# Where the split weights and the activations begin within a line of 256 bytes of SBUF

## The chip, the cores and the metric

The kernel runs on one core of a Trainium2 chip. The time is device microseconds of one execution of the whole program. Before the change three runs took 1443.82, 1444.29 and 1444.64 us, so the median is 1444.29 us.

## The reference, cut to what matters

A decoder layer of 256 tokens and 2048 channels, all in float32: one input projection that feeds sliding-window attention and a state-space mixer side by side, an output projection, and a convolved, gated feed-forward layer.

```python
def reference(x, ...):
    h = x
    h = h + _hybrid_mixer(_rmsnorm(h, norm_mix), w_in, ..., w_out)
    h = h + _conv_ffn(_rmsnorm(h, norm_ffn), w_up, ffn_conv_w, ffn_conv_b, w_down)
    return _rmsnorm(h, norm_final)

def _hybrid_mixer(xn, w_in, ..., w_out):
    proj = xn @ w_in                      # [256, 2048] @ [2048, 9248]
    ...
    return jnp.concatenate([attn, y], axis=-1) @ w_out      # [256, 4096] @ [4096, 2048]

def _conv_ffn(hn, w_up, ffn_conv_w, ffn_conv_b, w_down):
    u = _causal_dwconv(hn @ w_up, ffn_conv_w, ffn_conv_b)   # [256, 2048] @ [2048, 11264]
    gate, val = u[..., :D_FF], u[..., D_FF:]
    return (jax.nn.silu(gate) * val) @ w_down               # [256, 5632] @ [5632, 2048]
```

## The kernel before, in words

Nearly all of the work is four large products of activations with weights, and each is made of three: an operand is split into a rounded part `hi` and the rest `lo` (type float32r), and hi x hi, hi x lo and lo x hi are summed in PSUM (`mm3`, lines 155 to 158). The weights come from HBM by SP's queue in blocks of 128 x 2048 floats into one of three buffers `raw` (`pieces`, line 77). Each half of a block is then split (`split`, line 67): ScalarE (ACT) casts it to `hi` (line 70), VectorE (DVE), or for one half in four GpSimd (POOL), subtracts `hi` from `raw` into `lo` (line 72). `hi` and `lo` have four buffers each, taken in turn, 4352 bytes a partition, of which a half of 1024 floats uses 4096.

A matmul has a stationary operand of 128 columns, loaded by a weight load ahead of it, and a moving operand of up to 512 columns. There are two forms:

- `gemm_tok` (line 174) has the activations stationary and the weights moving, 512 columns at a time. It serves the keys and the time steps (`w_kd`, in two cuts of 256 and 288 columns), the values, the queries and z (activations in `xT`), the output projection (`attT`, then `yT`) and, written out separately (`down`, line 835), the down projection (`gs`). Leaving `w_kd` aside these are 864 matmuls on `xT` (9 products of 16 row tiles x 2 token tiles x 3), 768 on `attT` and `yT` and 1056 on `gs`.
- `gemm_chan` (line 200) has the weights stationary and the activations moving. In the state space (lines 217 to 219) it makes 1536 matmuls of 256 columns of `xT`. In the up projection (lines 223 and 225) a 512-column matmul on `hi` (the activation's `hi` and `lo` beside each other) and a 256-column one on `lo` make a pair; there are 1408 pairs on `h2T`, which has the buffer of `xT`.

An activation's tile holds for each of 16 row tiles a `hi` of 256 floats and a `lo` of 256 floats. Every slice that a matmul of a large product reads begins a multiple of 256 bytes after the start of its tile, except the second row tile of a part of `w_kd`, which begins 2176 bytes after the first. So an operand's place within a line of 256 bytes is that of its tile.

The tiles' starts are set by the pools, which allot a partition's bytes in the order of the calls. In the built program, in bytes past a multiple of 256: `xT` and `h2T` 128; all buffers of `hi` and `lo` 96 (their spacing, 4352, is 17 x 256); `attT`, `yT` and `gs` 96; in attention `vs` 160 and `pt` and `po` 96.

The mixers' smaller steps (attention, the state space's chunks) are called in between the large products' turns (`later`, `step`), and a scheduler of the tile framework sets the order on each engine from its own estimate of time.

Of the kernel before, what the change touches and what calls it, by code (L numbers as in the profile page):

```python
# [36 lines left out]
RAWW = 4 * KDT  # L37
# [10 lines left out]
def hymba(ctx, tc, x, xt, w_kd, w_in, w_out, w_up, w_down, par, vecs, gfin, con, out):  # L48
# [16 lines left out]
    share = [0, 0]  # L65

    def split(raw, o, n):
        hi = wp.tile([P, RAWW // 2], F32R, tag="hi", name="hi", bufs=4)
        lo = wp.tile([P, RAWW // 2], F32R, tag="lo", name="lo", bufs=4)
# [7 lines left out]
    def pieces(src, width, parts, load=None, work=None):  # L77
        """the parts of a block's splits; load, work: what goes before a part's load and split."""
        raw = wp.tile([P, RAWW], F32, tag="raw", name="raw", bufs=3)
        n = width // parts  # L80
        if load:
            for h in range(parts):
                load(h)
                SY.dma_start(out=raw[:, h * n : (h + 1) * n], in_=src[:, h * n : (h + 1) * n])
        else:
            SY.dma_start(out=raw[:, :width], in_=src)
        out = []
        for h in range(parts):
            if work:
                work(h)  # L90
            out.append(split(raw, h * n, n))
        return out

    xT = cp.tile([P, NKT, 2, S], F32R, tag="xT", name="xT")
# [22 lines left out]
    def rstd(dst, ss, n):  # L117
        """dst = (ss / n + EPS) ** -0.5, a column for each of the token tiles."""
# [4 lines left out]
    def rows_of(dst, r):  # L123
        """dst[p, t] = r of token t, on every partition."""
# [7 lines left out]
    def split_T(dst, kt, src, g, view=lambda a: a):  # L132
        """dst[:, kt] = the two parts of src * g."""
# [6 lines left out]
    def transpose_split(src, ct0, dst, kt0, n, gbase):  # L140
        """src [tokens, t, channels] to the parts of its transpose, n channel tiles times their weights."""
# [18 lines left out]
    # work beside the large products: steps that come up so many turns after they are called for  # L160
# [13 lines left out]
    def gemm_tok(blocks, actT, evac, width=2048, cuts=((0, 512),), tag="acc", parts_of=None):  # L174
        """out[token, column]: activations stationary, weights moving."""
# [24 lines left out]
    def gemm_chan(blocks, actT, evac, tag="acc", wide=True):  # L200
        """out[channel, token]: weights stationary, activations moving; wide: in two sums for evac to add."""
# [29 lines left out]
    def conv(dst, b, rB, wcol, bias, taps, wide):  # L231
        """dst = causal convolution over tokens of b * rB, channels on partitions."""
# [15 lines left out]
    attT = mixctx.enter_context(tc.tile_pool(name="mp0", bufs=1)).tile([P, NKT, 2, S], F32R, name="attT")  # L248

    # =========== attention ===========  # L250
# [675 lines left out]
def _cols(v):  # L926
    """[..., n * P] to [P, ... * n]."""
    return v.reshape(-1, P).T
# [61 lines left out]
```

## Time and profile before

| | |
|---|---|
| median of three runs | 1444.29 us (1443.82 to 1444.64) |
| span of the profiled execution, first to last instruction | 1442.0 us |
| TensorE busy (matmuls) | 1406.4 us of the span |
| weight loads / VectorE / ScalarE / GpSimd busy | 1231.3 / 989.6 / 772.0 / 269.4 us |
| HBM read | 259.92 MB, 182 GB/s over the span |

The profile gives no time of the profiled execution but its span, so the time that lies around the span is taken as 1444.29 - 1442.0 = 2.3 us. Stages by TensorE's lines: keys, values and queries from 6 us, attention's and the state space's products to 525 us, output projection to 703 us, up projection to 1193 us, down projection to 1432 us. In a row of the profile a matmul's duration is longer than the time until the next one starts, because matmuls overlap; the difference of two starts is called its spacing here.

### The profile page before, as it was taken

To read this page: it belongs to the slowest core of one execution; us is meant where nothing else is said; L and a number is where in the kernel's file an instruction comes from. 1 tells how busy PE (TensorE), PEld (TensorE's weight loads), DVE (VectorE), ACT (ScalarE), POOL (GpSimd) and SP (SyncE) were. 2 spreads that over 40 slices of the span, in tenths; PEclk is the share of its full clock that TensorE was granted. 3 is DMA by queue.
4 is the path that set the end of the run, shared out by engine and by line. 5 is a ranking of instruction groups with operands and counts; after the bars stand their busy time and mean duration, and the time that the engine had idled before them with its cause. 6 is when DMAs were issued, how large, how long until landed. Compare 5 with 4: busy or idle time off the path is not lost.

```text
span 1442.0 us, 20476 instructions
## 1 busy us (share of the span) xinstructions
PE 1406.4 (98%) x7925; PEld 1231.3 (85%) x7925; DVE 989.6 (69%) x1454; ACT 772.0 (54%) x1209; POOL 269.4 (19%) x187
## 2 busy tenths in 40 slices
PE   8999999899999999999999999999999999999997
PEld 8888888789999988888888888888888888888886
DVE  6579999788685755555577776867767767545555
ACT  6565677456555554344465554555555554444444
POOL 0124544443434330000000111101111001000001
PEclk9999999999999999999999999999999999999999
DMA  8643333445545456554655555555555455555552
GB/s 317 237 166 125 117 118 117 140 153 190 182 172 186 155 175 257 179 201 175 226 180 195 187 181 200 187 193 190 190 187 192 176 204 190 190 204 182 197 199 94
DMA packets 40561, 263.37 MB, mean 183 GB/s; under 512 B 4608, under 2 KB 5248, under 8 KB 10640
## 3 DMA queue, kind: packets, MB, share of 16 engines
q1 hardware_dynamic: 38560, 254.69, 49.4%
q0 software_dynamic: 1904, 7.37, 1.8%
q8 instruction: 62, 1.02, 0.3%
q14 instruction: 35, 0.29, 0.1%
HBM read 259.92 MB, written 2.13 MB: 182 GB/s over the span
## 4 chain that ended last, share of the span: by engine, by line
PE 81%; DVE 10%; ACT 3%; issue 3%; POOL 1%; DMA 1%; SPq 0%; DVEq 0%; POOLq 0%; ACTq 0%
PE acc L225 11%; PE aux L225 11%; PE acc L158 10%; PE acc L157 10%; PE acc L156 10%; PE aux L223 6%; PE acc L223 6%; PE aux L156 3%; PE aux L157 3%; PE aux L158 3%; DVE lo L72 3%; DVE u L242 2%; PE acc L219 1%; PE acc L218 1%; PE acc L217 1%
## 5 line engine op out<-in xcount | busy, mean ns | idle before, releaser
L72 DVE TENSOR_TENSOR lo<-raw,hi 128x1024 fp32r<-128x1024 f32 (+2 forms) x442 | 550.0, 1250 | 348.9 <-ACT hi L70 348.3
L70 ACT CAST hi<-raw 128x1024 fp32r<-128x1024 f32 (+2 forms) x474 | 492.2, 1047 | 451.7 <-PE acc L158 135.3
L225 PE MATMUL acc<-h2T,hi 128*128 128x512 f32 x704 | 243.4, 391 | 0.0
L225 PE MATMUL aux<-h2T,hi 128*128 128x512 f32 x704 | 243.0, 391 | 0.0
L223 PE MATMUL aux<-h2T,lo 128*128 128x256 f32 x704 | 191.1, 282 | 0.0
L223 PE MATMUL acc<-h2T,lo 128*128 128x256 f32 x704 | 191.0, 282 | 0.0
L225 PEld LDWEIGHTS aux<-h2T,hi 128*128 128x128 f32 x704 | 129.8, 188 | 24.6
L225 PEld LDWEIGHTS acc<-h2T,hi 128*128 128x128 f32 x704 | 129.8, 188 | 24.5
L217 PE MATMUL acc<-xT,hi 128*128 128x256 f32 x512 | 145.4, 285 | 0.0
L218 PE MATMUL acc<-xT,hi 128*128 128x256 f32 x512 | 144.7, 283 | 0.0
L219 PE MATMUL acc<-xT,lo 128*128 128x256 f32 x512 | 143.9, 282 | 0.0
L817 POOL TENSOR_TENSOR gT<-gate,cv 128x256 f32<-128x256 f32 x44 | 61.2, 1392 | 434.5 <-DVE cv L242 424.0
L223 PEld LDWEIGHTS acc<-h2T,lo 128*128 128x128 f32 x704 | 132.9, 189 | 3.9
L223 PEld LDWEIGHTS aux<-h2T,lo 128*128 128x128 f32 x704 | 132.9, 189 | 3.8
L156 PE MATMUL acc<-hi,xT 128*128 128x512 f32 (+1 forms) x320 | 117.6, 387 | 6.4 <-ACT hi L70 5.7
L157 PE MATMUL acc<-lo,xT 128*128 128x512 f32 (+1 forms) x320 | 122.5, 386 | 0.6 <-DVE lo L72 0.6
L158 PE MATMUL acc<-hi,xT 128*128 128x512 f32 (+1 forms) x320 | 122.1, 384 | 0.0
L72 POOL TENSOR_TENSOR lo<-raw,hi 128x1024 fp32r<-128x1024 f32 x32 | 82.7, 2584 | 146.3 <-ACT hi L70 146.2
L218 PEld LDWEIGHTS acc<-xT,hi 128*128 128x128 f32 x512 | 97.1, 190 | 0.4
L217 PEld LDWEIGHTS acc<-xT,hi 128*128 128x128 f32 x512 | 97.0, 190 | 0.4
L219 PEld LDWEIGHTS acc<-xT,lo 128*128 128x128 f32 x512 | 96.9, 190 | 0.2
L156 PEld LDWEIGHTS acc<-hi,xT 128*128 128x128 f32 x320 | 60.4, 195 | 17.1 <-ACT hi L70 5.7
(224 smaller groups left out, 2421.9 us busy)
## 6 DMA issues: line engine op xcount, KB each, us to landing
raw<-in_w_up SPq DMA_DIRECT2D x88, 1024.0 KB, 4.8
raw<-in_w_in SPq DMA_DIRECT2D x68, 1024.0 KB, 4.8
raw<-in_w_down SPq DMA_DIRECT2D x44, 1024.0 KB, 4.8
raw<-in_w_out SPq DMA_DIRECT2D x32, 1024.0 KB, 4.8
e<-acs_d POOLq DMA_DIRECT2D x8, 512.0 KB, 6.2
raw<-in_w_kd SPq DMA_DIRECT2D x6, 544.0 KB, 7.8
x_r<-in_x SPq DMA_DIRECT2D x2, 1024.0 KB, 5.3
h<-in_x POOLq DMA_DIRECT2D x4, 512.0 KB, 7.5
```

The costliest lines, as they stand in the source:

```text
L70: A.copy(out=hi[:, :n], in_=raw[:, o : o + n])
L72: (G if share[0] and share[1] % share[0] == 0 else V).tensor_tensor(out=lo[:, :n], in0=raw[:, o : o + n], in1=hi[:, :n].bitcast(F32), op=A ...
L156: PE.matmul(out=o, lhsT=lh, rhs=rh, start=first, stop=False)
L157: PE.matmul(out=o, lhsT=lh, rhs=rl, start=False, stop=False)
L158: PE.matmul(out=o, lhsT=ll, rhs=rh, start=False, stop=last)
L217: PE.matmul(out=b[ct][:, :S], lhsT=wh, rhs=rh, start=kt == 0, stop=False)
L218: PE.matmul(out=b[ct][:, :S], lhsT=wh, rhs=actT[:, kt, 1, :], start=False, stop=False)
L219: PE.matmul(out=b[ct][:, :S], lhsT=wl, rhs=rh, start=False, stop=end)
L223: PE.matmul(out=b[ct][:, :S], lhsT=wl, rhs=rh, start=False, stop=False)
L225: PE.matmul(out=b[ct], lhsT=wh, rhs=actT[:, kt, :, :], start=kt == 0, stop=end)
L242: V.scalar_tensor_tensor(out=dst[:, j:], in0=u[:, : S - j], scalar=wcol(taps - 1 - j), in1=dst[:, j:], op0=ALU.mult, op1=ALU.add,)
L817: G.tensor_tensor(out=gT[:, i, :], in0=gate[:, ct, :], in1=dst, op=ALU.mult)
```

## The change

The tiles of the large products get places of their own. A new helper `placed` allots a tile on a line of 256 bytes with some bytes to spare and returns the part that begins `at` bytes in. The four buffers of `hi` (and of `lo`) become four tiles of one buffer each, at 0, 64, 128 and 192; `hi` and `lo` of the same half have the same place. `xT` begins at 0, and `h2T`, `attT`, `yT` and `gs` at 32.

```diff
-RAWW = 4 * KDT
+RAWW = 2048
+HALF = 1024
+LINE = 256
+
+W_AT, X_AT, H_AT, M_AT = (0, 64, 128, 192), 0, 32, 32
...
+    def placed(pool, n, at, tag, **kw):
+        tl = pool.tile([P, n + at // 4], F32R, tag=tag, align_bytes=LINE, **kw)
+        return tl[:, at // 4 : at // 4 + n]
+
     def split(raw, o, n):
-        hi = wp.tile([P, RAWW // 2], F32R, tag="hi", name="hi", bufs=4)
-        lo = wp.tile([P, RAWW // 2], F32R, tag="lo", name="lo", bufs=4)
+        j = share[1] % len(W_AT)
+        hi = placed(wp, HALF, W_AT[j], f"hi{j}", name="hi", bufs=1)
+        lo = placed(wp, HALF, W_AT[j], f"lo{j}", name="lo", bufs=1)
...
     def pieces(src, width, parts, load=None, work=None):
-        raw = wp.tile([P, RAWW], F32, tag="raw", name="raw", bufs=3)
         n = width // parts
+        per = RAWW // n
+        raws = [wp.tile([P, RAWW], F32, tag="raw", name="raw", bufs=3) for _ in range(-(-parts // per))]
+        at = lambda h: raws[h // per][:, h % per * n : (h % per + 1) * n]
...
-    xT = cp.tile([P, NKT, 2, S], F32R, tag="xT", name="xT")
+    def acts(pool, at, **kw):
+        return placed(pool, NKT * 2 * S, at, **kw).rearrange("p (k i s) -> p k i s", i=2, s=S)
+
+    xT = acts(cp, X_AT, tag="xT", name="xT")
...
     def parts_kd(i, src):
-        n = 1 if i == 0 else 2
+        n = 1
...
-        return pieces(src, 4 * KDT, 4 if i == 0 else 2, load, work)
+        return pieces(src, 4 * KDT, 4, load, work)
...
-        ta, tb, tcc, td = (ap.tile([P, nd], F32, tag=f"sp{i}", name=f"sp{i}") for i in range(4))
+        ta, tb, tcc, td = (ap.tile([P, nd], F32, tag=t, name=t, bufs=1) for t in ("sp0", "sp1", "rpa", "rpb"))
...
-        gs = fp.tile([P, 2, S], F32R, tag="gs", name="gs", bufs=4)
+        gs = placed(fp, 2 * S, M_AT, "gs", name="gs", bufs=4).rearrange("p (i s) -> p i s", i=2)
```

`attT` and `yT` change like `gs` (`M_AT`), `h2T` like `xT` (`H_AT`). A buffer of `raw` shrinks from 2176 to 2048 floats and one of `hi` or `lo` from 1088 to 1024, which makes room. For this the blocks of `w_kd`, of 2176 floats, are now all loaded and split in quarters of 544, three in one `raw` buffer and the fourth in another; before, the first block came in quarters and the other three in halves. Two small tiles of `steps_dt` share buffers with those of `rope`.

In the built program the tiles stand where the change says: the buffers of `hi` and `lo` at 0, 64, 128 and 192, `xT` at 0, `h2T`, `attT`, `yT` and `gs` at 32; `vs` is now at 96, and `pt` and `po` at 32.

The places that matter for a matmul are those of its moving operand and of the next stationary operand, whose load runs beside it. Below, the **distance** is the first minus the second, in bytes, taken around the line of 256:

| form | distance before | distances after, by buffer of the weights |
|---|---|---|
| `gemm_tok` on `xT`, 512 columns | 224 | 0, 64, 128, 192 |
| `gemm_tok` on `attT`, `yT`; `down` on `gs`, 512 columns | 0 | 224, 32, 96, 160 |
| `gemm_chan` on `xT`, 256 columns | 32 | 0, 192, 128, 64 |
| `gemm_chan` on `h2T`, 512 and 256 columns | 32 | 32, 224, 160, 96 |
| attention's values: `pt` or `po` moving, `vs` stationary, 256 columns | 192 | 192 |

The order of the instructions changes in the first third of the program. On SP's queue, at the second block of `w_kd` (`xraw` takes four row tiles of the input, `raw` the weights; a number tells the buffer's use), before:

```order
L84 DMA raw_105<-in_w_kd 128x544
L312 DMA xraw_92<-in_xt 128x512
L84 DMA raw_186<-in_w_kd 128x1088
L312 DMA xraw_92<-in_xt 128x512
L84 DMA raw_186<-in_w_kd 128x1088
L319 DMA con_t_70<-in_con 128x576
```

and now, at its last two quarters:

```order
L327 DMA xraw_92<-in_xt 128x256
L96 DMA raw_187<-in_w_kd 128x544
L327 DMA xraw_92<-in_xt 128x256
L96 DMA raw_188<-in_w_kd 128x544
L334 DMA con_t_70<-in_con 128x576
```

Each half became two quarters, and the fourth quarter goes to a `raw` buffer of its own. On TensorE, at the first queries (`aux <- con_t, q_t` are their transposes, put in between the matmuls of the next product), before:

```order
L156 MATMUL acc_784<-hi_791,xT_69 128x512
L442 MATMUL aux_833<-con_t_70,q_t_615 128x128 x4
L157 MATMUL acc_784<-lo_792,xT_69 128x512
L158 MATMUL acc_784<-hi_791,xT_69 128x512
L156 MATMUL acc_783<-hi_850,xT_69 128x512
```

and now:

```order
L171 MATMUL acc_824<-hi_831,xT_69 128x512
L172 MATMUL acc_824<-lo_832,xT_69 128x512
L457 MATMUL aux_873<-con_t_70,q_t_655 128x128 x4
L173 MATMUL acc_824<-hi_831,xT_69 128x512
L171 MATMUL acc_823<-hi_890,xT_69 128x512
```

The transposes moved back by one matmul. There are more such moves, by one to a few matmuls, up to the last products of the state space; from the output projection on, TensorE's order is the same.

## Rows read from the trace of the kernel before

**Rows 1.** The page: span, engines' busy time, shares of the chain that ended last.

```profile
span 1442.0 us, 20476 instructions
...
PE 1406.4 (98%) x7925; PEld 1231.3 (85%) x7925; DVE 989.6 (69%) x1454; ACT 772.0 (54%) x1209; POOL 269.4 (19%) x187
...
PE 81%; DVE 10%; ACT 3%; issue 3%; POOL 1%; DMA 1%; SPq 0%; DVEq 0%; POOLq 0%; ACTq 0%
```

**Rows 2.** Windows: us, busy us (instructions) by engine, clock, DMA share, GB/s.

```profile
160.00:200.00 40.00, 38.47 (x291) 35.97 (x291) 36.38 (x64) 25.84 (x65) 17.10 (x12) 1.00 0.35 123
200.00:240.00 40.00, 34.80 (x276) 33.80 (x274) 35.88 (x62) 27.05 (x59) 13.82 (x9) 0.96 0.26 91
800.00:840.00 40.00, 40.00 (x233) 35.35 (x232) 28.49 (x43) 22.37 (x34) 4.66 (x4) 1.00 0.55 202
1280.00:1320.00 40.00, 40.00 (x178) 33.15 (x177) 19.93 (x23) 18.25 (x23) 0.00 (x0) 1.00 0.54 197
```

**Rows 3.** PE's waits, 80 to 300 us: releaser, us in all, times, longest.

```profile
PE aux L156 <- DVE pt L524: 7.1, 6, 2.1
PE aux L157 <- DVE pt L515: 3.3, 1, 3.3
```

**Rows 4.** By line: matmuls' ns min/median/max, first to last start, shapes.

```profile
L157 PE MATMUL acc<-lo,gs x176: 389/389/395, 1193.4 to 1426.6; 128*128 128x512 f32 x176
...
L157 PE MATMUL acc<-lo,yT x128: 389/389/389, 547.9 to 702.3; 128*128 128x512 f32 x128
...
L157 PE MATMUL aux<-lo,xT x32: 389/395/397, 34.0 to 56.4; 128*128 128x512 f32 x32
...
L156 PE MATMUL aux<-po,vs x16: 276/278/415, 121.9 to 280.2; 128*128 128x256 f32 x16
...
L217 PE MATMUL acc<-xT,hi x512: 274/280/471, 173.3 to 498.6; 128*128 128x256 f32 x171
...
L225 PE MATMUL acc<-h2T,hi x704: 390/390/481, 702.8 to 1170.7; 128*128 128x512 f32 x176
...
L223 PE MATMUL acc<-h2T,lo x704: 277/282/363, 703.0 to 1170.6; 128*128 128x256 f32 x176
```

**Rows 5.** Timeline, PE, down projection: start us, us, instruction; 14 spacings.

```profile
1299.71 0.39 PE L158 MATMUL acc<-hi,gs 128*128 128x512 f32 x1
...
1302.88 0.39 PE L157 MATMUL acc<-lo,gs 128*128 128x512 f32 x1
```

**Rows 6.** Timeline, PE, values' projection: 6 spacings.

```profile
34.02 0.40 PE L157 MATMUL aux<-lo,xT 128*128 128x512 f32 x1
...
35.42 0.40 PE L158 MATMUL aux<-hi,xT 128*128 128x512 f32 x1
```

**Rows 7.** Timeline, PE, up projection: 16 pairs of matmuls.

```profile
800.02 0.39 PE L225 MATMUL acc<-h2T,hi 128*128 128x512 f32 x1
...
805.57 0.39 PE L225 MATMUL acc<-h2T,hi 128*128 128x512 f32 x1
```

**Rows 8.** Timeline, PE, attention's values: 8 spacings.

```profile
164.79 0.28 PE L158 MATMUL aux<-pt,vs 128*128 128x256 f32 x1
...
165.69 0.28 PE L157 MATMUL aux<-po,vs 128*128 128x256 f32 x1
```

**Rows 9.** Timeline, PE, first microseconds: one spacing.

```profile
7.65 0.41 PE L157 MATMUL acc<-lo,xT 128*128 128x256 f32 x1
7.86 0.41 PE L158 MATMUL acc<-hi,xT 128*128 128x256 f32 x1
```

**Rows 10.** PE's waits, 0 to 40 us.

```profile
PE acc L157 <- DVE lo L72: 0.6, 1, 0.6
```

**Rows 11.** Timeline, SP queue: first and last load of w_kd.

```profile
1.66 0.42 SPq L84 DMA_DIRECT2D raw<-in_w_kd  x1
...
16.48 0.43 SPq L84 DMA_DIRECT2D raw<-in_w_kd  x1
```

More of the change, by code (lines that the diff above doesn't have):

```diff
@@ L83, in pieces @@
                 load(h)
-                SY.dma_start(out=raw[:, h * n : (h + 1) * n], in_=src[:, h * n : (h + 1) * n])
+                SY.dma_start(out=at(h), in_=src[:, h * n : (h + 1) * n])
         else:
-            SY.dma_start(out=raw[:, :width], in_=src)
+            SY.dma_start(out=raws[0][:, :width], in_=src)
         out = []
@@ L90, in pieces @@
                 work(h)
-            out.append(split(raw, h * n, n))
+            out.append(split(at(h), 0, n))
         return out
-    xT = cp.tile([P, NKT, 2, S], F32R, tag="xT", name="xT")
+    def acts(pool, at, **kw):
+        return placed(pool, NKT * 2 * S, at, **kw).rearrange("p (k i s) -> p k i s", i=2, s=S)
+    xT = acts(cp, X_AT, tag="xT", name="xT")
     con_t = cp.tile([P, NCON], F32, name="con_t")
@@ L247, in hymba @@
     mixctx = ExitStack()
-    attT = mixctx.enter_context(tc.tile_pool(name="mp0", bufs=1)).tile([P, NKT, 2, S], F32R, name="attT")
+    attT = acts(mixctx.enter_context(tc.tile_pool(name="mp0", bufs=1)), M_AT, tag="attT", name="attT")
     apctx = ExitStack()
@@ L688, in open_sp @@
         apctx.close()
-        yT = mixctx.enter_context(tc.tile_pool(name="mp1", bufs=1)).tile([P, NKT, 2, S], F32R, name="yT")
+        yT = acts(mixctx.enter_context(tc.tile_pool(name="mp1", bufs=1)), M_AT, tag="yT", name="yT")
         sp = spctx.enter_context(tc.tile_pool(name="sp", bufs=1))
@@ L755, in hymba @@
     hp = h2 = None
-    h2T = cp.tile([P, NKT, 2, S], F32R, tag="xT", name="h2T")
+    h2T = acts(cp, H_AT, tag="xT", name="h2T")
     ss2 = cp.tile([P, NT, 4], F32, name="ss2")
```

## The prediction

> **What bounds the kernel now.** I read the page first: TensorE is busy for 1406.4 of 1442.0 us, and 81% of the chain that ended last is its own [rows 1]. Then the windows: from 800 to 840 us and from 1280 to 1320 us TensorE is busy without a gap, VectorE and ScalarE far from it; only in attention (160 to 240 us) does TensorE stand still for some us in 40, with VectorE at 36 of 40 [rows 2], and there the longest waits are for VectorE's `pt`, 7.1 and 3.3 us in all [rows 3]. The granted clock is 1.00 in the two later windows. So what a change of places can move is the spacing of TensorE's matmuls.
>
> The spacings follow from starts: in the down projection (3.17 us over 14) 226 ns for 512 columns [rows 5]; on `xT` (1.40 us over 6) 233 ns for the same 512 columns [rows 6]; in the up projection (5.55 us over 16) 347 ns for a pair of 512 and 256 columns [rows 7]; in attention's values (0.90 us over 8) 113 ns for 256 columns [rows 8]. A matmul's duration is its spacing plus 162 ns (389 - 226 in the first, 395 - 233 in the second), so medians of durations compare as spacings [rows 4]. The reader is to see there that one shape has several: 512 columns take 389 on `gs` and `yT`, 390 on `h2T`, 395 on `xT`; 256 columns take 278 at attention's values (276 where nothing disturbs them), 280 on `xT`, 282 on `h2T`. They hardly vary inside a line (389/389/389 for `yT`), while the other engines work on and off beside them. What differs between the lines is the distance: 0 for `gs` and `yT`, 224 for `xT` stationary, 32 for `xT` or `h2T` moving, 192 for the values. Hence my reading: the place does count, by up to 6 ns a matmul, and between TensorE's own two reads, not against other engines.
>
> **The change, part by part.** Each product gets four distances in turn, a quarter of its matmuls each.
>
> *512 columns on `xT`, 864 matmuls.* 224 becomes 0, 64, 128, 192, all multiples of 64. The two rows at such distances (0: 389; 192: 276) are the shortest of their widths, so I take 389 for 395: 864 x 6 = 5.2 us. The queries' 384 stand in or near the stretch where TensorE waits for VectorE [rows 2, 3]; I let half of theirs (1.2 us) go into a longer wait for VectorE, which is late next. **-4.0 us.**
>
> *256 columns on `xT`, 1536 matmuls.* 32 becomes 0, 192, 128, 64. At 192 the row says 276 against 280; I take that for two places of four and no change for the others: 1536 / 2 x 4 ns. **-3.1 us.**
>
> *Pairs on `h2T`, 1408.* One place keeps 32. A pair of the shortest durations (389 and 276) would be 7 ns less than 390 and 282. Again two places of four: 1408 / 2 x 7 ns. **-4.9 us.** Nothing hides it, TensorE has no gap there.
>
> *512 columns on `attT`, `yT`, `gs`, 1824 matmuls.* They have the shortest row already. At 224, a quarter of them, I charge `xT`'s 395: 456 x 6 ns. At 32, 96 and 160 nothing. **+2.7 us.**
>
> *Bounds of these prices.* Downwards: in the first microseconds the same matmuls run at half the pace, 0.21 us for 256 columns with their loads [rows 9]; half of it, 105 ns, and 210 for 512 is then an estimate of what columns alone cost at the later pace. At that every product would lose its excess: 864 x 23 + 1536 x 13 + 1408 x 32 + 1824 x 16 ns = 114 us. Upwards: every 512 at 395 and every 256 at 282: 1824 x 6 + 1408 x 5 + 1536 x 2 ns = +21 us. The present rows lie close to the upper end; but values inside the rows seen, 6 ns apart, are what I trust.
>
> *The start, `w_kd`.* Twelve more loads on SP's queue (six halves of weights and six of `xraw` become twelve each), 0.42 us to issue one [rows 11]: 5 us if the queue were the limit. The last of them was issued at 16.5 us [rows 11], and the next product's matmuls start only at 34 us [rows 4], so they are covered. Fewer `raw` buffers run ahead; if that cover went, the queue would wait for VectorE's splits and TensorE for the load. Smaller parts come sooner: the one stall after the start, 0.6 us on `lo` [rows 10], may go. I take 0, between -0.6 and +5.
>
> *Order and shared buffers.* From the output projection on the order stands. The moves in attention can give or take what TensorE waits there for `pt`, 7 us either way at most [rows 3]; I take 0. `steps_dt` and `rope` write their shared buffers on VectorE alone, in order: 0. The splits keep their size, and the spare bytes cost nothing.
>
> **Sum:** -4.0 - 3.1 - 4.9 + 2.7 = -9.3 us. The profiled span of 1442.0 becomes 1432.7; with the 2.3 us around it, that is the median of 1444.3 becoming **1435 us**, 0.6% faster. A change under 0.2% (2.9 us) can't be told from none.
>
> **Rivals.**
>
> *Odd multiples of 32 cost everywhere (slower).* For it: the rows at 32 and 224 (390, 282, 280, 395) all lie above those at 0 and 192 (389, 276). The change gives odd multiples to `attT`, `yT`, `gs` and `h2T`, most of the columns, even ones to `xT`. Priced by rows: 1824 at the mean of 390 and 395, +3.5 ns each, +6.4 us; the 512s on `h2T` at that mean, +2.5 ns x 1408, +3.5 us; against -4.0 and -3.1 on `xT`. That is +2.8 us, and with the 256s on `h2T` or the start 1 or 2 us more: 1449. It decides from 1.5 ns a matmul on the 1824 and nothing gained on `h2T`. Against it: the lines differ in more than the parity, and distances 96 and 160 stand in no row of 512 columns.
>
> *The places mean nothing (same).* The 6 ns would come from the form of the product and not from the start: `xT` stationary is 395 and `gs` 389 in the same form, which speaks against it, but only two tiles show it. Then only the start's terms are left: 1444. [...]
>
> *The conflicts go for the most part (much faster).* A fixed distance repeats one pattern for a whole stage; if four places break it, the excess over the columns could halve: half of 114 us, 1387. The rows show no matmul near that, 113 ns against 105 being the nearest.
>
> That the change doesn't do what it says is excluded: the built program has the tiles at those places.
>
> [...]
>
> **How the numbers follow.** The forecast has 0.38, slower by odd multiples 0.31, same 0.21, much faster 0.10. So faster 0.48, same 0.21, slower 0.31. The range reaches down to 1412, where the pairs and `xT` win at all places and some beyond the shortest rows (-32 us), and up to 1456, half the upper bound of 21 us and a little for the start; it leaves out most of the fourth case and the far end of the second.
>
> **What would show it.** In the new profile, the durations by line: 512 columns on `xT` at 389 and not 395; 256 columns on `xT` with a part at 276; on `h2T` 282 falling for some buffers; on `gs` a quarter at 395 and the rest at 389. If `gs` and `h2T` go up while `xT` goes down, the second case is right; if all stay, the third. TensorE's waits in attention tell whether the order took part. I am wrong if the time moves while all these durations stay.

## The result and the profile after

The changed kernel takes 1453.76 us (median of 4 runs, 1452.30 to 1456.40), the kernel before 1444.05 us (4 runs, 1443.36 to 1444.64) beside it: a ratio of 1.0069, 95% interval 1.0055 to 1.0083. It is **0.7% slower**, 9.7 us, where I had forecast 9.3 us less. The time lies inside the range, the direction is wrong.

First the page of the changed kernel: span, busy times, shares of the chain that ended last.

```profile
span 1451.5 us, 20529 instructions
...
PE 1416.8 (98%) x7925; PEld 1225.4 (84%) x7925; DVE 997.3 (69%) x1460; ACT 771.7 (53%) x1215; POOL 270.8 (19%) x187
...
PE 80%; DVE 9%; ACT 3%; DMA 3%; POOL 2%; issue 2%; SPq 0%; DVEq 0%; POOLq 0%; ACTq 0%
```

Against [rows 1] the span is 9.5 us longer and TensorE is busy 10.4 us longer with the same 7925 matmuls, while its share of the chain is the same within a point. So the matmuls themselves got longer, and no new wait took over.

The windows of the changed kernel (us, busy us and instructions by engine, granted clock, DMA share, GB/s):

```profile
200.00:240.00 40.00, 35.89 (x286) 34.27 (x285) 38.87 (x71) 28.20 (x69) 14.02 (x9) 1.00 0.31 112
800.00:840.00 40.00, 40.00 (x231) 35.03 (x230) 28.22 (x43) 22.17 (x34) 4.54 (x4) 1.00 0.56 198
1280.00:1320.00 40.00, 40.00 (x173) 32.17 (x172) 19.50 (x21) 17.57 (x22) 0.00 (x0) 1.00 0.53 190
```

The granted clock is 1.00 in all three, as it was in the two later ones of [rows 2]; from 200 to 240 us that had 0.96. In the down projection 173 matmuls fit into 40 us where 178 did, in the up projection 231 where 233 did; in this window of attention nothing is lost.

By line, for the changed kernel (matmuls' ns min/median/max, first to last start, shapes; L171 to L173 are the three products of `mm3`, L233 one of the 256-column products on `xT`, L238 and L240 the pair on `h2T`):

```profile
L172 PE MATMUL acc<-lo,gs x176: 391/396/401, 1195.9 to 1436.2; 128*128 128x512 f32 x176
...
L172 PE MATMUL acc<-lo,yT x128: 391/395/400, 543.0 to 701.6; 128*128 128x512 f32 x128
...
L172 PE MATMUL aux<-lo,xT x32: 388/394/499, 32.0 to 55.4; 128*128 128x512 f32 x32
...
L233 PE MATMUL acc<-xT,hi x512: 276/281/561, 166.9 to 493.5; 128*128 128x256 f32 x171
...
L238 PE MATMUL acc<-h2T,lo x704: 277/280/366, 702.3 to 1172.9; 128*128 128x256 f32 x176
...
L240 PE MATMUL acc<-h2T,hi x704: 389/392/480, 702.1 to 1173.1; 128*128 128x512 f32 x176
```

These rows answer to [rows 4] and hold the whole result. `gs` and `yT` went from 389 to 396 and 395, and not a quarter of them but all: even the minimum, 391, is above the old median. `xT` with 512 columns fell by 1 ns only. Of the pair one median rose by 2 ns and the other fell by 2, so its change has to be read from the length of its stage, which follows.

The rows also give two stage lengths that every run below is compared by. Between the first and the last start of the `gs` row lie 1029 matmuls (counted in the two traces; the order there stands in all kernels): 233.2 us before [rows 4], 240.3 now, that is 226.6 and 233.5 ns each. The row of L240 (L225 before) spans 2700 matmuls: 1343 pairs and 12 small matmuls of other tiles, here taken as 1350 pairs. That is 467.9 us before [rows 4], 471.0 now, 346.6 and 348.9 ns a pair. Worked out from the starts inside the pairs alone it would be 0.8 to 1 ns more in both kernels, so the figures serve to compare kernels.

The same spacing at one place, in the timeline of the changed kernel, down projection:

```profile
1299.79 0.40 PE L173 MATMUL acc<-hi,gs 128*128 128x512 f32 x1
...
1303.07 0.40 PE L172 MATMUL acc<-lo,gs 128*128 128x512 f32 x1
```

14 spacings in 3.28 us, 234 ns; [rows 5] had 226.

Two waits of TensorE in the changed kernel, from 0 to 40 us (the first is the start, until the first weights are split):

```profile
PE acc L171 <- ACT hi L80: 5.3, 1, 5.3
PE aux L172 <- DVE lo L82: 0.2, 1, 0.2
```

The stall of 0.6 us [rows 10] is gone and the values' projection begins at 32.0 us instead of 34.0 [rows 4].

### The profile page after: what moved, and what is told of

Its sections match the earlier page's. It is cut to its first block, busy times and chain, and to the rows that moved or that the text cites. A ratio compares the mean times of both kernels' runs of the same rounds, so it can differ in the third digit from the quotient of the medians.

```text
span 1451.5 us, 20529 instructions
## 1 busy us (share of the span) xinstructions
PE 1416.8 (98%) x7925; PEld 1225.4 (84%) x7925; DVE 997.3 (69%) x1460; ACT 771.7 (53%) x1215; POOL 270.8 (19%) x187
## 4 chain that ended last, share of the span: by engine, by line
PE 80%; DVE 9%; ACT 3%; DMA 3%; POOL 2%; issue 2%; SPq 0%; DVEq 0%; POOLq 0%; ACTq 0%
PE acc L240 11%; PE aux L240 11%; PE acc L173 9%; PE acc L171 9%; PE acc L172 9%; PE aux L238 6%; PE acc L238 6%; PE aux L172 3%; PE aux L173 3%; PE aux L171 3%; PE acc L234 3%; PE acc L233 3%; PE acc L232 3%; DVE lo L82 2%; ACT hi L80 1%
## 5 line engine op out<-in xcount | busy, mean ns | idle before, releaser
L82 DVE TENSOR_TENSOR lo<-raw,hi 128x1024 fp32r<-128x1024 f32 (+1 forms) x448 | 566.3, 1270 | 372.6 <-ACT hi L80 371.4
L80 ACT CAST hi<-raw 128x1024 fp32r<-128x1024 f32 (+1 forms) x480 | 491.9, 1033 | 465.1 <-PE aux L173 135.8
L240 PE MATMUL acc<-h2T,hi 128*128 128x512 f32 x704 | 244.9, 394 | 0.0
L240 PE MATMUL aux<-h2T,hi 128*128 128x512 f32 x704 | 244.6, 393 | 0.0
L238 PE MATMUL aux<-h2T,lo 128*128 128x256 f32 x704 | 190.3, 280 | 0.0
L238 PE MATMUL acc<-h2T,lo 128*128 128x256 f32 x704 | 190.2, 281 | 0.0
L240 PEld LDWEIGHTS aux<-h2T,hi 128*128 128x128 f32 x704 | 129.9, 188 | 26.5
L240 PEld LDWEIGHTS acc<-h2T,hi 128*128 128x128 f32 x704 | 129.8, 188 | 26.3
L233 PE MATMUL acc<-xT,hi 128*128 128x256 f32 x512 | 144.5, 284 | 0.0
L238 PEld LDWEIGHTS acc<-h2T,lo 128*128 128x128 f32 x704 | 132.6, 188 | 4.1
L238 PEld LDWEIGHTS aux<-h2T,lo 128*128 128x128 f32 x704 | 132.6, 188 | 4.0
L171 PE MATMUL acc<-hi,xT 128*128 128x512 f32 (+2 forms) x320 | 115.5, 381 | 5.3 <-ACT hi L80 5.3
L172 PE MATMUL acc<-lo,xT 128*128 128x512 f32 (+2 forms) x320 | 120.2, 380 | 0.0
L173 PE MATMUL acc<-hi,xT 128*128 128x512 f32 (+2 forms) x320 | 120.1, 378 | 0.0
L82 POOL TENSOR_TENSOR lo<-raw,hi 128x1024 fp32r<-128x1024 f32 x32 | 80.5, 2516 | 118.0 <-ACT hi L80 118.0
L233 PEld LDWEIGHTS acc<-xT,hi 128*128 128x128 f32 x512 | 97.3, 190 | 0.4
L171 PEld LDWEIGHTS acc<-hi,xT 128*128 128x128 f32 x320 | 59.4, 192 | 15.2 <-ACT hi L80 5.3
```

Of the source, the lines that this page charges most:

```text
L80: A.copy(out=hi[:, :n], in_=raw[:, o : o + n])
L82: (G if share[0] and share[1] % share[0] == 0 else V).tensor_tensor(out=lo[:, :n], in0=raw[:, o : o + n], in1=hi[:, :n].bitcast(F32), op=A ...
L171: PE.matmul(out=o, lhsT=lh, rhs=rh, start=first, stop=False)
L172: PE.matmul(out=o, lhsT=lh, rhs=rl, start=False, stop=False)
L173: PE.matmul(out=o, lhsT=ll, rhs=rh, start=False, stop=last)
L233: PE.matmul(out=b[ct][:, :S], lhsT=wh, rhs=actT[:, kt, 1, :], start=False, stop=False)
```

## The experiments

All edits are to the changed kernel, nearly all to the one line of places. "One place" means the same place for all four buffers of `hi` and `lo`, so that a form keeps one distance throughout. In all but m_at_0, fine16, fine16_again and two_16 one small tile of `steps_dt` moves to another buffer as well, which makes room:

```
-        ... for t in ("sp0", "sp1", "rpa", "rpb"))
+        ... for t in ("sp0", "s0", "rpa", "rpb"))
```

Where a result is a single run, the stages are compared and not the total, since runs of one program beside each other differed by up to 5 us.

### Are odd multiples of 32 the trouble, is any change of place, or only the same place good?

```
-W_AT, X_AT, H_AT, M_AT = (0, 64, 128, 192), 0, 32, 32
+W_AT, X_AT, H_AT, M_AT = (0, 64, 128, 192), 0, 32, 0       m_at_0
+W_AT, X_AT, H_AT, M_AT = (32, 96, 160, 224), 0, 32, 32     w_odd
```

> The changed kernel with attT, yT and gs at 0 in place of 32, so that their distances to the weights' buffers are 0, 64, 128 and 192 (all 1824 matmuls of 512 columns). Theory A (a distance that is an odd multiple of 32 costs 6 to 7 ns a matmul of 512 columns, a multiple of 64 nothing): spacing on these lines falls from 233 ns to 226.7 at all four places, 12 us less: span about 1439 us. Rival B (both operands have to begin off a multiple of 64, as they did at 96 and 96 before): spacing as on xT in the changed kernel, where both begin at multiples of 64: 230 to 232.6 ns, 2 to 6 us less: span about 1447. Rival C (only the same place, distance 0, is short): 226.7 for the buffer at 0 and 233 for the other three: 3 us less, about 1448.

> The changed kernel with the weights' buffers at 32, 96, 160 and 224 (one small tile of the time steps shares a buffer to make room). Distances to attT, yT, gs become 0, 64, 128, 192 with both operands off a multiple of 64; on h2T 0, 64, 128, 192 too; on xT they become odd multiples of 32. Theory A: 226.7 ns on attT, yT and gs at all four places (12 us less), the 512s on h2T at 227 or below against 231.6 (6 us less), xT back to 233 (1.5 us more): span about 1435. Rival B: the same on these lines, since both are off a multiple of 64. Rival C: only a quarter of each gains: about 1447.

Measured: 1450.73 and 1451.51 us. The down projection's row by line, in m_at_0:

```profile
L172 PE MATMUL acc<-lo,gs x176: 388/394/404, 1195.9 to 1433.7; 128*128 128x512 f32 x176
```

and in w_odd:

```profile
L172 PE MATMUL acc<-lo,gs x176: 388/394/404, 1196.7 to 1434.5; 128*128 128x512 f32 x176
```

Both have the distances 0, 64, 128, 192 on `gs`, from absolute places that differ by 32 bytes, and both take 237.8 us, 231.1 ns each: the absolute place does not matter, the distance does. (The next experiment says the same: 233.2 us for `gs` at 96 on 96 before, 233.3 at 0 on 0.) Sorted by distance, the spacings that can be worked out from the starts are 228.6, 230.4, 232.7 and 232.8 ns in m_at_0. So even multiples of 32 are not short as a group, and my rival's rule of odd and even falls with these two runs: only 0 is near the old 226.6, 64 somewhat above it, 128 and 192 are as long as the odd ones of the change.

### The rest of the change without its places

```
+W_AT, X_AT, H_AT, M_AT = (96, 96, 96, 96), 128, 128, 96    places_of_before
+W_AT, X_AT, H_AT, M_AT = (0, 0, 0, 0), 32, 32, 0           dist_of_before
```

Both give every form the distance that it had before; the second at other absolute places.

> The changed kernel with the places of the kernel before: all four weights' buffers at 96, xT and h2T at 128, attT, yT and gs at 96; the quarters of w_kd, the smaller buffers and the order stay as changed. If all of the loss is in the places: spacings of before (233.0, 226.7, 229.2 and 118.1, 116.9 ns) and a span of 1440 to 1443 us, the start 2 us earlier than before included. If the shape of the buffers or the order costs: 1446 or more.

> The changed program (quarters of w_kd, its order, its shared buffers) with one place for all weights, so that every product has the distance that it had before the change, but at other absolute places than before and than in places_of_before. Theory D (the distance alone): every spacing as before, 233.0 ns for 512 columns on xT, 116.9 for 256 with xT moving, 347.3 for a pair on h2T, 226.7 on attT, yT, gs; the output, up and down projections at 177.9, 490.4 and 239.5 us; what is left is the start and attention: 1439 to 1441, ratio 0.997 to 0.9985 against the kernel before. Theory F (the 3 us that one look at places_of_before was below the kernel before were scatter of the start, the quarters bring nothing): the same spacings, ratio 0.999 to 1.001. Theory A (absolute places count): spacings that differ from those of before by over 1 ns.

Measured: 1438.97 us in one run of places_of_before, and for dist_of_before 1439.21 us (median of 6, 1437.75 to 1441.89) against 1444.06 (median of 10): **0.9969, interval 0.9957 to 0.9980**. By line, dist_of_before:

```profile
L172 PE MATMUL acc<-lo,gs x176: 389/389/395, 1188.8 to 1422.1; 128*128 128x512 f32 x176
...
L172 PE MATMUL aux<-lo,xT x32: 392/396/503, 32.4 to 57.0; 128*128 128x512 f32 x32
...
L240 PE MATMUL acc<-h2T,hi x704: 390/390/477, 698.2 to 1166.1; 128*128 128x512 f32 x176
```

The lengths, 233.3 and 467.9 us, are those of before. So the rest of the change gains 4.8 us, and the places lose 14.55 (1453.76 - 1439.21; the small tile's other buffer is in this difference, but the stages behind attention, where it is no longer used, are 15.2 longer by themselves: 177.8, 490.4 and 239.5 us here, 182.6, 493.5 and 246.8 in the changed kernel, by the starts of each product). The gain lies early: comparing starts in the two profiles, the first matmul comes 0.5 us sooner, the products on `w_kd` take 1.8 us less, and from the values to the output projection it is 2.35 us less. No run has the quarters alone, without the smaller buffers and the new order, so the cause is not shown part by part. For the last 2.35 us there is another candidate, TensorE's clock. From 120 to 320 us, in windows of 40, the granted clock was 0.96, 1.00, 0.96, 0.91 and 0.91 in the kernel before, and 1.00, 1.00, 1.00, 0.96 and 0.96 in dist_of_before: about 20 us at the lower of its two levels (0.50) against 7. The kernel before's two runs at a mean clock of 0.995 took 1441.66 and 1442.71 us, its three at 0.989 1446.71 to 1447.48 (one at 0.943, with 1442.69, stands apart). Beside the runs at 0.995 dist_of_before, at 0.994 to 0.996, gains about 3 us and not 4.8.

### Does the changing of places cost, or the distance itself?

Three kernels with one place, so that nothing changes from part to part:

```
+W_AT, X_AT, H_AT, M_AT = (0, 0, 0, 0), 0, 0, 0             all_at_0
+W_AT, X_AT, H_AT, M_AT = (0, 0, 0, 0), 192, 64, 192        one_w_64
+W_AT, X_AT, H_AT, M_AT = (0, 0, 0, 0), 64, 128, 128        one_w_192
```

> The changed kernel with every large operand at 0: one place for all weights' buffers, distance 0 everywhere. Theory D (with the activations stationary, a matmul of 512 columns takes 226.7 ns at distance 0 and 229 to 233.5 at any other; a part's first matmuls after a change of distance take up to 10 ns more): xT's 512s settle at 226.7 as gs and yT do, against 233.1; on gs and yT 226.7 as in the kernel before. With activations moving, by the shares of the runs so far at distance 0: 119.4 ns for 256 columns on xT (116.9 at 32), pairs on h2T 349 (347 at 32): span about 1437 + 3.8 + 2.8 - 4, 1440 us. Theory E (only the going from place to place costs, any one place is as good as another): all lines at the values of the kernel before or lower, 226.7 on xT too, 1432.

> All weights' buffers at 0; xT, attT, yT, gs at 192 (distance 64 where they stand still), h2T at 64 (distance 64 where it moves), xT moving at distance 192. Theory D: 229 ns (the pattern 226, 229, 232 that the buffer at 64 settled to) on xT, gs, attT, yT: 864 x 4 ns less and 1824 x 2.3 ns more than in places_of_before, nearly nothing in sum; 256 columns on xT 113 to 117. Theory E: 226.7 on all of them.

> All weights' buffers at 0; xT at 64 (distance 192 standing still, 64 moving), attT, yT and gs at 128 (distance 128), h2T at 128 (distance 128). Theory D: 233 ns on gs, attT, yT and on xT's 512s: as slow as the changed kernel there, 12 us more than places_of_before, though no buffer changes its place. Theory E: 226.7 on all, as fast as places_of_before.

Measured: 1447.18, 1454.96 and 1459.24 us (the kernel before beside them 1444.92). By line, all_at_0, with distance 0 everywhere:

```profile
L172 PE MATMUL acc<-lo,gs x176: 389/389/389, 1197.0 to 1430.2; 128*128 128x512 f32 x176
...
L233 PE MATMUL acc<-xT,hi x512: 274/283/562, 165.7 to 494.4; 128*128 128x256 f32 x171
...
L240 PE MATMUL acc<-h2T,hi x704: 389/398/478, 698.1 to 1173.9; 128*128 128x512 f32 x176
```

one_w_192, with 128 on `gs` and on `h2T`:

```profile
L172 PE MATMUL acc<-lo,gs x176: 391/393/399, 1202.1 to 1442.2; 128*128 128x512 f32 x176
...
L240 PE MATMUL acc<-h2T,hi x704: 386/396/478, 706.5 to 1179.2; 128*128 128x512 f32 x176
```

one_w_64, with 64 on both and 192 where `xT` moves:

```profile
L172 PE MATMUL acc<-lo,gs x176: 388/388/394, 1202.5 to 1438.0; 128*128 128x512 f32 x176
...
L233 PE MATMUL acc<-xT,hi x512: 276/276/562, 172.1 to 498.5; 128*128 128x256 f32 x171
...
L240 PE MATMUL acc<-h2T,hi x704: 388/397/481, 703.8 to 1179.4; 128*128 128x512 f32 x176
```

One place with 128 on `gs` takes 240.1 us, 233.3 ns each, with no changing at all: as much as the four places. So the distance itself costs. And the same distance is not good for all forms: 0 is best for `gs` (233.2 us) and the worst seen for the pair (475.8 against 467.9); 192 is long with `xT` stationary (233.2 ns) and the shortest for 256 columns with `xT` moving (276 against 280).

### The other distances, and a better choice

```
+W_AT, X_AT, H_AT, M_AT = (0, 0, 0, 0), 16, 16, 240         one_w_16
+W_AT, X_AT, H_AT, M_AT = (0, 0, 0, 0), 192, 192, 0         h_192
+W_AT, X_AT, H_AT, M_AT = (0, 0, 0, 0), 240, 240, 0         h_240
+W_AT, X_AT, H_AT, M_AT = (0, 0, 0, 0), 160, 96, 224        m_32
+W_AT, X_AT, H_AT, M_AT = (0, 0, 0, 0), 96, 224, 96         m_160
```

> All weights' buffers at 0, attT, yT and gs at 240 (distance 16), xT and h2T at 16 (240 standing still, 16 moving). If the grain of the places is 32 bytes, distance 16 gives 226.7 as distance 0 does or 233 as 32 does; a third value says that the grain is finer. It also tells whether the granted clock of 0.85 in fine16 comes with places that are multiples of 16: 0.99 here says that it does not.

> One place for all weights; the distances are 64 for 512 columns on the stationary xT, 192 where xT moves, 192 for the pairs on h2T, 0 on attT, yT, gs. Theory D (the distance alone sets the spacing, nothing else does): from the earlier runs with one place, xT at 229.5 +- 0.5 ns, 256 columns with xT moving at 114.6 +- 0.5, attT/yT/gs at 226.7; the output and down projections at 177.9 and 239.5 us as before. For the pairs at 192 no run with one place has a row. D1 (the pair follows the narrow products, whose shortest row is at 192): about 227 + 114.6, 341 to 343 ns, the up projection 482 to 484 us and the whole near 1424. D2 (the pair's 512 follows the 512 on stationary activations, 233 at 192): 350 to 353 ns, the up projection 494 to 498, the whole 1437 to 1441. Theory E (only a change of place costs, a fixed place is always at its shortest): all of them as short as anywhere, the whole near 1424, but one_w_192 has spoken against it.

> One place for all weights; the distances are 16 for 512 columns on xT, 240 where xT moves, 240 for the pairs on h2T, 0 on attT, yT, gs. Theory D: xT at 228 +- 0.5 ns (its row at 16 from attT and yT), attT/yT/gs at 226.7. 256 columns with xT moving at 240: no row yet; between 114.6 (192) and 119.7 (0). Pairs at 240: D1 (like the narrow products, near their row at 192): 341 to 344, the up projection 482 to 485; D2 (near the row at 0): 350 to 353, the up projection 494 to 498. The whole 1424 to 1428 with D1, 1438 to 1445 with D2.

> One place for all weights; the distances are 32 for attT, yT, gs, 96 for 512 columns on the stationary xT, 160 where xT moves, 96 for the pairs on h2T: those of the change that no run has alone. In the changed kernel 32 and 96 took 233.3 and 234.1 ns on gs. Theory S (the distances themselves are long): the same alone, 233 +- 1 ns on gs (the down projection 245.5 to 247.5 us) and on xT. Theory T (they are short alone, and the change from part to part makes them long, as two_16 showed 3 ns of it): 227 to 230 on gs (240 to 243 us). Pairs at 96: 351 to 353, like the rows at 64 and 128 beside it, the up projection 495 to 498 us. The whole: S 1457 to 1461, T 1450 to 1455.

> As m_32, with the distances 160 for attT, yT, gs and for 512 columns on xT, 96 where xT moves, 224 for the pairs on h2T. Theory S: 233 +- 1 ns on gs (in the changed kernel 233.4), the down projection 245.5 to 247.5 us. Theory T: 227 to 230, 240 to 243 us. Pairs at 224: 350 to 353 like 192 and 240 beside it, the up projection 493 to 498. The whole: S 1455 to 1461, T 1448 to 1455.

Measured: 1439.73, 1443.91, 1444.83, 1460.43 and 1461.20 us. By line, one_w_16, with 16 on `gs` and `h2T`:

```profile
L172 PE MATMUL acc<-lo,gs x176: 387/390/392, 1187.8 to 1422.7; 128*128 128x512 f32 x176
...
L240 PE MATMUL acc<-h2T,hi x704: 387/388/483, 697.3 to 1165.1; 128*128 128x512 f32 x176
```

h_192 (0 on `gs`, 192 on `h2T`):

```profile
L240 PE MATMUL acc<-h2T,hi x704: 388/397/508, 695.2 to 1170.6; 128*128 128x512 f32 x176
```

h_240 (240 on `h2T`):

```profile
L240 PE MATMUL acc<-h2T,hi x704: 388/397/477, 697.1 to 1171.5; 128*128 128x512 f32 x176
```

m_32 (32 on `gs`, 96 on `h2T`):

```profile
L172 PE MATMUL acc<-lo,gs x176: 392/395/398, 1203.3 to 1443.4; 128*128 128x512 f32 x176
...
L240 PE MATMUL acc<-h2T,hi x704: 389/393/485, 708.3 to 1180.4; 128*128 128x512 f32 x176
```

m_160 (160 on `gs`, 224 on `h2T`):

```profile
L172 PE MATMUL acc<-lo,gs x176: 392/397/401, 1203.1 to 1444.2; 128*128 128x512 f32 x176
...
L240 PE MATMUL acc<-h2T,hi x704: 388/396/482, 704.7 to 1180.1; 128*128 128x512 f32 x176
```

Theory S holds: alone, 32 takes 240.1 us on `gs` (233.3 ns) and 160 takes 241.1 (234.3 ns). For the pairs the hope that they follow the narrow products (D1) falls with h_192 and h_240. Together, in ns, from kernels with one place; for `gs` and the pairs by the rows' stage lengths over 1029 and 1350, for the two forms on `xT` (marked *) the mean of the spacings between starts, leaving out those at a wait. Where 512 columns have both, `xT` agrees with `gs` within 0.6 ns (16, 64, 160), except at 0, where `xT` has 228.5:

| distance | 512 columns, activations stationary | 256 columns, `xT` moving * | pair on `h2T` |
|---|---|---|---|
| 0 | 226.6 | 119.7 | 352.4 |
| 16 | 228.3 | 117.7 | 346.5 |
| 32 | 233.3 | 116.8 | 346.6 |
| 64 | 228.9 | 117.6 | 352.3 |
| 96 | 233.6 * | 119.9 | 349.7 |
| 128 | 233.3 | | 350.1 |
| 160 | 234.3 | 118.2 | |
| 192 | 233.2 * | 114.6 to 115.2 | 352.1 |
| 224 | 233.1 * | | 352.1 |
| 240 | 231.7 * | 117.2 | 351.4 |

From it the best choice that the program's four knobs allow among these: 0 for `M_AT`, 32 for `H_AT`, and 192 for `X_AT` (64 with `xT` stationary, 192 with it moving).

```
+W_AT, X_AT, H_AT, M_AT = (0, 0, 0, 0), 192, 32, 0          best
```

> As dist_of_before, with X_AT at 192: 512 columns on the stationary xT at a distance of 64 instead of 224, 256 columns with xT moving at 192 instead of 32; pairs at 32 and attT, yT, gs at 0 as before. Theory D: xT 229.4 for 233.0 on 864 matmuls, -3.1 us; 115.0 for 116.9 on 1536, -2.9 us; the later stages as before. Together 5 to 6.5 us below dist_of_before: 1433 to 1436, ratio 0.9925 to 0.995 against the kernel before. Rival: what attention's products gain is spent waiting for VectorE's pt and for the loads, and the time stays within 2 us of dist_of_before.

Measured: 1437.97 us (median of 5, 1436.86 to 1440.28), **0.9957 of the kernel before, interval 0.9943 to 0.9970**. That beats both kernels, but its median is 1.2 us below dist_of_before and not 5 to 6.5, and the runs of the two overlap: the rival's number held. The matmuls did what the table says (229.5 and 115.2 ns in the profiled execution), which is worth 5.4 us from the end of the values' projection to the output projection. That stretch took 463.1 us in both profiles, so the time did not follow there. Waits of TensorE in dist_of_before, 60 to 520 us:

```profile
PE aux L171 <- DVE pt L539: 6.4, 5, 3.8
PE aux L162 <- DVE y L694: 3.4, 3, 1.6
...
PE aux L172 <- DVE pt L530: 1.0, 1, 1.0
PE aux L171 <- ACT pt L529: 1.0, 1, 1.0
```

The same waits in best:

```profile
PE aux L171 <- DVE pt L539: 7.3, 6, 3.8
PE aux L162 <- DVE y L694: 3.8, 3, 1.7
...
PE aux L172 <- DVE pt L530: 1.5, 2, 1.0
PE aux L171 <- ACT pt L529: 1.3, 1, 1.3
```

These four grew from 11.8 to 13.9 us, all waits of that stretch from 19.4 to 22.1: 2.7 us came back as waiting for other engines, as the rival said. The clock took its part as well: from 250 to 300 us the mean granted clock was 0.90 in best and 0.93 in dist_of_before, that is about 10 against 7 us at the level of 0.50. And this one execution (1440.28 us, the highest of its five) lost time earlier, as the window from 41 to 51 us shows in best:

```profile
41.00:51.00 10.00, 7.69 (x27) 5.64 (x26) 7.07 (x20) 8.31 (x14) 0.70 (x1) 0.83 0.85 310
```

and in dist_of_before:

```profile
41.00:51.00 10.00, 8.37 (x37) 6.21 (x36) 6.93 (x19) 8.66 (x14) 0.70 (x1) 1.00 0.83 307
```

In best TensorE stood still for 2.3 us of ten, 2.2 of them in one wait for VectorE (`diag`, L143; 1.5 us in dist_of_before). After it, from 46 to 49 us, the granted clock was 0.50, with matmuls starting 0.43 us apart instead of 0.23; ten fewer were started in the window. In h_192, which has the same places up to the output projection, that projection begins at 517.35 us, against 521.58 in best and 520.38 in dist_of_before. So one execution with these places did win 3 us. How the other four of best went is not known; they have no profile.

### What does the change of place itself cost, and what is the low clock of fine16?

```
+W_AT, X_AT, H_AT, M_AT = (0, 16, 32, 48), 0, 0, 0          fine16, fine16_again
+W_AT, X_AT, H_AT, M_AT = (0, 16, 0, 16), 0, 0, 0           two_16
```

> The changed kernel with the weights' buffers at 0, 16, 32 and 48 and all activations at 0: distances 0, 16, 32 and 48 for weights moving, 0, 240, 224 and 208 for activations moving, told apart by buffer in one profile. Theory A: with 512 columns 226.7 at 0 and 233 at 32; at 16 and 48 either of the two if places of 32 bytes matter, a third value if the grain is 16 bytes. Rival B: 230 at 0 (both at multiples of 64), 233 at 32. Rival C: 226.7 at 0 and 233 at the other three.

> The same kernel as fine16, whose only look ran at a granted clock of 0.85 from 10 us to its end, so that it says nothing of places. Theory P (places 16 apart bring the low clock): 0.85 again, spacings near 248 ns, 1540 to 1550 us, ratio 1.07. Theory X (the low clock belonged to that one execution): clock 0.99 and more; then the distances count, 0, 16, 32, 48 in turn for attT, yT, gs (226.7, 228 and twice up to 233: the down projection 242 to 244 us) and 0, 240, 224, 208 for the pairs (350 to 353 ns: the up projection 494 to 499 us), the whole 1447 to 1457, ratio 1.003 to 1.009.

> Two places 16 apart for the weights, taken in turn, all activations at 0; the distances are 0 and 16 for 512 columns with stationary activations, 0 and 240 for the others. By the rows with one place, 226.7 and 228 ns on attT, yT, gs: if a change of place cost nothing, 227.4, the output and down projections at 178.4 and 240.2 us; what they take beyond that is the price of the change of place itself (in m_at_0 a part's first four to six matmuls after a change took up to 10 ns more; at that rate 20 to 40 ns for each part of 12, the down projection 242 to 243.5 us). Pairs: 352 to 353, the up projection 497 to 499. The whole 1445 to 1451 at a clock of 0.99; theory P of fine16 gives 0.85 and 1540 or more.

The one run of fine16 took 1547.92 us. Its window in the down projection:

```profile
1280.00:1320.00 40.00, 40.00 (x161) 30.61 (x160) 20.05 (x23) 16.63 (x21) 0.79 (x2) 0.85 0.51 181
```

The granted clock was 0.85 there, neither of the levels 0.50 and 1.00 of the other profiles, and 0.84 in the mean from 10 to 50 us; it fell at about 10 us, with TensorE already at work. The same program under the name fine16_again took 1451.48 us (median of 4, ratio 1.0052, 1.0035 to 1.0069) at a clock of 1.00 in the down projection. So theory X holds: the low clock belonged to that one execution, and its 7% is not a price of places.

What the low clock does to places shows in the same row of the two. In fine16:

```profile
L172 PE MATMUL acc<-lo,gs x176: 404/411/432, 1272.7 to 1530.8; 128*128 128x512 f32 x176
```

and in fine16_again:

```profile
L172 PE MATMUL acc<-lo,gs x176: 387/394/400, 1194.0 to 1432.8; 128*128 128x512 f32 x176
```

At a clock of 1.00 fine16_again takes 232.1 ns in the mean and, sorted by distance, 230.3 at 0, 231.4 at 16, 233.6 at 32 and 232.7 at 48. At 0.85 fine16 takes 250.8, and all four distances lie between 250.7 and 251.1: there the distance made no difference. The short stretches at 0.50 agree, with 426 to 427 ns (two to six spacings each) for 512 columns at a distance of 64 (best), 96 (m_32) and 224 (dist_of_before). Times the granted clock, 250.8 and 427 are both 213 ns. At 1.00 the shortest in the table is 226.6, so by this estimate the distances act on the 13 to 21 ns that come on top of 213 at the full clock.

two_16 took 1451.14 us. By line:

```profile
L172 PE MATMUL acc<-lo,gs x176: 389/394/398, 1197.1 to 1434.1; 128*128 128x512 f32 x176
```

237.0 us, 230.3 ns each, while its two distances alone take 226.6 and 228.3, 227.5 in the mean. Changing costs 2.8 ns a matmul here, 3.0 us over the 1056 of the stage. Its timeline shows where (the first part of 12 matmuls is at distance 0, the second at 16):

```profile
1301.96 0.39 PE L171 MATMUL acc<-hi,gs 128*128 128x512 f32 x1
...
1303.35 0.39 PE L171 MATMUL aux<-hi,gs 128*128 128x512 f32 x1
...
1304.71 0.39 PE L171 MATMUL acc<-hi,gs 128*128 128x512 f32 x1
...
1307.49 0.39 PE L171 MATMUL acc<-hi,gs 128*128 128x512 f32 x1
```

The first six spacings after the change to distance 0 take 1.39 us, the next six 1.36: the matmuls fall back into the short rhythm after half a dozen. The 12 at distance 16 take 2.78 us, 231.7 ns each: they do not find their short rhythm (228.3) within a part. The price of changing differs from case to case: 0.6 ns in m_at_0 (231.1 against 230.5, the mean of its four distances alone), and nothing in the changed kernel on `gs`, as the next section works out.

## Why the prediction was wrong

*That TensorE's spacing bounds the kernel, and that the start of a tile moves it through the distance,* was right. From the output projection to the end TensorE waited for no other engine, and the three stages there explain the loss against dist_of_before: by the table and the rows, 1824 matmuls at 233.5 instead of 226.7 ns are 12.4 us, 1408 pairs at 348.9 instead of 346.6 are 3.2 us. The two kernels with nothing changed but where tiles start show it, by 226.6 against 233.3 ns on `gs` (dist_of_before and m_32). Whether it is TensorE's own two reads that get in each other's way, as I read the rows, is not shown. The 210 ns for 512 columns, my estimate from [rows 9] of what the columns alone cost, was reached nowhere: 226.6 is the shortest of this width in the table, at a clock of 1.00.

*512 columns on `attT`, `yT`, `gs`, forecast +2.7 us, measured +12.4.* **This is the step that failed.** I charged 6 ns to the quarter at distance 224 and wrote "at 32, 96 and 160 nothing". The runs show 233.3 ns at 32 and 234.3 at 160 on `gs`, and 233.6 at 96 and 233.1 at 224 on `xT`: all four are long, and their mean, 233.6, is what the changed kernel has. No changing of places is needed to explain it. I had a row for 0 and a row for 224 of this width, and filled the gap between them with the better one; the row at 32 that I had was of another form. The upper bound of this term, all 1824 at the price of `xT`, was nearly the right number (10.9 us).

*512 columns on `xT`, forecast -4.0, measured about -1.5.* The spacing went from 233.0 to 231.3, not to 227. I took all multiples of 64 as good; alone, 0 takes 226.6 to 228.5 (`gs`, `xT`), 64 takes 229, but 128 and 192 take 233. The row at 192 that I leaned on had 256 columns and other operands.

*256 columns on `xT`, forecast -3.1, measured about +1.7.* 118.0 ns for 116.9 on 1536 matmuls. 192 is indeed short (115 alone), but 0 is long (119.7), where I had written "no change"; and among four places 192 gave only about 117. The 276 that I set against 280 was moreover the least of its row, and 280 a median; the least of `xT`'s own row is 274 [rows 4].

*Pairs on `h2T`, forecast -4.9, measured +3.2.* Of the distances that were run alone (160 was not) only 16 is as short as 32, which the kernel had; 96 and 224 take 3 and 5.5 ns more. I had read the 390 and 282 of this row as the price of a bad place; it was the best place of this form. The sign that I had named for a gain, 282 falling, came (280), while the pair got longer: for the pair the medians of durations do not compare as spacings.

*`w_kd`'s start and the order, forecast 0 within -0.6 and +5, measured -4.8.* The loads stayed covered, as I said: behind the start (5.3 us) TensorE's one wait up to 40 us is for `lo`, 0.2 us. But I had bounded the gain by the one stall of 0.6 us, and the first products and the values' projection came 2.3 us forward. A bound from a single wait was too narrow. Of the rest, up to the output projection, I had no term for the clock: the 0.96 of 200 to 240 us stood in [rows 2], and less time at its lower level may be part of the gain.

*Together:* 12.4 + 3.2 - 1.5 + 1.7 - 4.8 = +11.0 against +9.7 measured; of the rest, 0.4 us is that the three later stages took 15.2 us more and not 15.6, and some 1 us is attention's stage, which ended 0.8 us earlier than in dist_of_before though its spacings say 0.2 later. Against the forecast the terms missed by 9.7, 8.1, 2.5, 4.8 and -4.8 us. Behind the first four stands the same step: a distance without a row in its own form was priced by the better row at hand or by a row of another form. That the time still lies in the range is luck in part: the three later stages lost 15.2 us, more than the 12 that the range allowed, and the start gave 4.8 back.

*The rivals.* "Odd multiples of 32 cost everywhere" had the right side and the nearest time (1449), but not the right rule: with 512 columns 128 (on `gs`) and 192 (on `xT`) are as long. "The places mean nothing" falls with dist_of_before against the changed kernel. "The conflicts go" falls altogether.

What stays open is why a distance of 0, 16 or 64 is short and the others long, why it is otherwise when the weights stand, and why 512 columns show it at the full clock alone: the runs give the table, not the mechanism. Nor do they tell the next stationary operand from the one in use, since both lie in tiles with the same place. Distances that are no multiples of 16 were not tried.

## What to carry to other kernels

Look at the spacing of successive matmuls of one shape, form by form: where it differs, the difference of the two operands' starts within a line of 256 bytes may be the cause. Here it was worth up to 3.4% of the 512-column matmuls with activations stationary (226.6 to 234.3 ns), 4.6% of the 256-column ones on `xT` (114.6 to 119.9) and 1.7% of the pairs (346.5 to 352.4). Keep one place for each operand and choose it for each form by measuring that place alone; rotating through places gave about the mean of good and bad here (233.5 ns for 233.6 on `gs` in the changed kernel), plus a price of changing of 0, 0.6 and 2.8 ns a matmul (changed kernel, m_at_0, two_16). A price seen in one form (which operand stands, how many columns) was not the price of another (distance 0 is 226.6 ns and the shortest on `gs`, 352.4 and among the longest for the pair), and a gain in a stage that waits for another engine need not be a gain in time (5.4 us by the spacings of best, with 463.1 us for the stretch in both profiles). Before putting down a few microseconds to a change, compare the granted clock of the two profiles window by window (from 120 to 320 us about 20 against 7 us at 0.50, before and in dist_of_before).

## What was not expected of the hardware

The order of good distances turns around between forms: 0 is the shortest with activations stationary (226.6 ns) and among the longest for the pair with weights stationary (352.4 against 346.5). A product has more than one rhythm at the same distance: at 16 it runs at 228.3 ns for a whole stage when nothing changes, and at 231.7 when it comes from another distance every 12 matmuls. At a lower granted clock the distance made no difference to 512 columns with activations stationary: 250.7 to 251.1 ns at 0, 16, 32 and 48 with 0.85, 426 to 427 at 64, 96 and 224 with 0.50. And one execution, fine16, ran from 10 us to its end at a granted clock of about 0.85 (0.848 in the mean), which the same program did not show again: 0.994 to 0.996 in the four of fine16_again.
